# Layer 0's mixer in a two-layer decoder: seven products taken to seven block products each, and decays with a bias per head

## The chip, the cores and the metric

The kernel runs on one core of a Trainium2 chip. The metric is device time in microseconds (us) of one execution, the median of several. The engines are named as in the profile: PE is TensorE's matrix multiplication (PEld its weight loads), DVE is VectorE, ACT is ScalarE, POOL is GpSimd, and SP is SyncE, which here issues DMA transfers only. The engines run side by side, each working through its own instructions in order, and wait for each other through semaphores.

## The reference, cut to what matters

Two layers work on 512 tokens of width 1024. Each is a half-step SwiGLU, a mixer, and another half-step SwiGLU. Layer 0's mixer is the one that the change touches: one input projection `w_in` feeds a Mamba-2 group (z, x, B, C, dt) and an mLSTM group (q, k, v, an output gate and two scalar gates), and one output projection takes both results.

```python
def hybrid_mixer(h, w_in, conv_w, ...):
    z, xbc, dt_raw, qm, km, vm, om, ig, fg = split_cols(h @ w_in, HY_SPLITS)
    xbc = jax.nn.silu(causal_dwconv(xbc, conv_w, conv_b))
    xs, bm, cm = split_cols(xbc, (1024, 256, 256))
    dt = jax.nn.softplus(dt_raw + dt_bias)
    y = ssd_chunked(xs, dt, -jnp.exp(a_log), bm, cm, 128) + xs * d_skip
    y = rms_norm((y * jax.nn.silu(z)) in 2 groups of 512, ssd_norm)
    hm = mlstm_chunked(qm, km, vm, ig + igate_bias, fg + fgate_bias, 128)
    hm = rms_norm(hm per head, mlstm_norm) * jax.nn.sigmoid(om)
    return jnp.concatenate([y, hm], -1) @ w_out

# inside ssd_chunked, per chunk of 128 tokens and per head; acs is the running sum of dt * A
Lm = jnp.exp(jnp.where(mask, acs[t] - acs[s], -inf))     # decay from token s to token t
# inside mlstm_chunked
S = (q . k) * jnp.exp(Dm - m_t);  w_inter = jnp.exp(inter - m_t)
```

z, v and the output gate are 1024 columns wide, q and k 512, x with B and C 1536. Everything is float32.

## The kernel before

**Products in three passes.** A float32 factor is split into a rounded high part and the rest (`split`: ACT copies the high part, DVE subtracts it from the source to get the low part), and a product is three matmuls (`mm3`, lines 274 to 279): high times high, high times low, low times high. `form` (line 257) does this for a block of weights: `raw` (line 250) loads a block of 128 x 1024 floats from SP into one of four buffers, and `form` writes its two parts into one of five buffers (`rings`). All of ACT's copies there stand on line 239 of the profile, all of DVE's subtractions on line 242. In the other stages there is a second way (lines 529 to 531): ACT writes the negated high part, a DMA issued by POOL adds the source to it, and ACT writes the high part; this keeps DVE out of it.

**Block products elsewhere.** The SwiGLU stages form most of their products by Winograd's variant of Strassen's scheme: both factors are cut into two by two blocks, and seven products of blocks (`seven`) take the place of eight, at the price of sums and differences of blocks ahead and behind. A block product here is 256 columns by 256 tokens over 512 rows, in matmuls of 256 columns.

**Layer 0's mixer, `hybrid`.** It has two interleavings (`weave`, which issues steps of a second stream between steps of the first) and is then ordered by the framework's scheduler, which fixes each engine's order when the program is built:

- `gates` (the scalar gates and everything derived from them) beside `conv`: six pairs of column groups of x, B and C. Each group takes 24 matmuls of 512 columns (`gemm_feat`), a multiplication of the result by the row of norms `rrow` on DVE (line 1022), the first step of the convolution on POOL, three more on DVE, and Silu on ACT.
- `ssd`, the Mamba recurrence over four chunks and four quarters of the heads, beside `projections`: q and k by columns (`gemm_feat`, line 973 takes them out of PSUM), then v and the output gate by tokens (`gemm_tok`, four banks of PSUM, ACT takes them out with Sigmoid for the gate). `decays` loads a row of running sums (`rows_from`), subtracts a column of them on DVE (line 1244), masks on POOL (line 1245), takes the exponential on ACT (line 1249), and multiplies by C B^T on DVE (line 1250), one quarter ahead.
- `mlstm` beside `gate`: z by columns (line 1046 multiplies by `rrow`), Silu, the product with the Mamba result, and its norm. `mlstm` forms its weights in the same manner (lines 1322 and 1324 subtract) and multiplies the gate by the result head by head (line 1357) and by its norm (line 1381).

Then `project` multiplies the 16 chunks of both results by `w_out` and starts the following SwiGLU. Every engine has one queue; a weight load waits on SP for its buffer, and a sum waits on POOL for ACT's copy.

Of the kernel before, what the change touches and what calls it, by code (L numbers as in the profile page):

```python
# [16 lines left out]
P = 128  # L17
# [27 lines left out]
NMIX = dict(mix0=10, mix1=15)  # L45
# [168 lines left out]
class Trunk:  # L214
# [21 lines left out]
    def split(self, hi, lo, src, eng="act"):  # L236
        nc = self.nc
        if eng == "act":
            nc.scalar.activation(hi, src, AF.Copy)
        else:  # L240
            nc.vector.tensor_copy(hi, src)
        nc.vector.tensor_tensor(lo, src, hi.bitcast(F32), op=ALU.subtract)
# [14 lines left out]
    def form(self, raw):  # L257
# [5 lines left out]
        if self.stage == "mix1":  # L263
# [7 lines left out]
    def wload(self, src):  # L271

        n = src.shape[0] // P
        for k in range(0, n, 4):
            yield self.form(self.raw(src[k * P : (k + 4) * P].rearrange("(k p) n -> p k n", p=P), 4, 256))
# [163 lines left out]

    def spread(self, cols, n, name):  # L440
# [10 lines left out]
    def rows_from(self, src, name):  # L451

        rows = self.tmp.tile([P, 4, P], F32, name=name, tag="rows", bufs=4)
        self.nc.sync.dma_start(rows, src.rearrange("n p -> (n p)").partition_broadcast(P).rearrange("q (n p) -> q n p", p=P))
        return rows
# [316 lines left out]
    def prep_later(self, which, k, last, squares=True, half=None):  # L772
# [5 lines left out]
        if k == 0 and not half:  # L778
            self.which = which
            self.xgn = [[Lazy(lambda: self.part.tile([P, 4, T], F32R, name="xgn", tag="xg")) for _ in range(2)] for _ in range(2)]  # L780
            squares4 = Lazy(lambda: self.tmp.tile([P, 4, T], F32, name="ssq", tag="ssq", bufs=1))
# [165 lines left out]
    def hybrid(self, nxt):  # L947
# [6 lines left out]
        weave(  # L954
            self.gates(w, ((0, DT0, 16), (16, F0, 4), (20, I0, 4)), g),
            chain(*(self.conv(w, X0, cp, xs, bc) for cp in (4, 5, 0, 1, 2, 3))),
            1.0,
        )

        q, k = self.slot("q"), self.slot("k")  # L960
        v = self.tmp.tile([P, 2, 2, 4, 257], F32, name="v", tag="v", bufs=1)
        v = [v[:, i] for i in range(2)]
        og = []

        def projections():
            for t, c0, sc in ((q, Q0, 128 ** -0.5), (k, K0, 1.0)):
                for cp in range(2):
                    W = self.wload(w[:, c0 + cp * 256 : c0 + cp * 256 + 256])
                    W = list(W)
                    for m in range(2):  # L970
                        ps = self.mmps("pqk")
                        self.gemm_feat(ps, W, m)
                        self.mark = nc.vector.scalar_tensor_tensor(
                            t[:, 2 * cp + m], ps, sc, self.rrow, op0=ALU.mult, op1=ALU.mult
                        )
                        yield
            for t in v:
                with self.tc.issue_after(self.mark.ins):
                    nc.vector.memset(t[:, :, :, 256:257], 1.0)
            for h in (0, 2):  # L980
                yield from self.gemm_tok(w, V0 + h * 256, 512, lambda b, ps, h=h: nc.scalar.activation(
                    v[b // 2][:, b % 2, h : h + 2, 0:256], ps.rearrange("p (h n) -> p h n", h=2), AF.Copy,
                    scale=self.rcol[:, b : b + 1]))
            og.extend(self.slot("og", F32, (2, 4, 256)) for _ in range(2))
            for h in (0, 2):
                yield from self.gemm_tok(w, O0 + h * 256, 512, lambda b, ps, h=h: nc.scalar.activation(
                    og[b // 2][:, b % 2, h : h + 2], ps.rearrange("p (h n) -> p h n", h=2), AF.Sigmoid,
                    scale=self.rcol[:, b : b + 1]))

        weave(self.ssd(xs, bc, g), projections(), 1.35)  # L990

        hid = [None] * 16

        def mlstm():
            yield from self.mlstm(q, k, v, og, g)
            hh, hl = self.feat("hh", KC, F32R), self.feat("hl", KC, F32R)
            for c in range(KC):
                pt = self.aux("pht", (T,))
                for b in range(NB):
                    nc.tensor.transpose(  # L1000
                        pt[:, b * P : (b + 1) * P], og[b // 2][:, b % 2, c // 2, (c % 2) * P : (c % 2 + 1) * P],
                        self.ident,
                    )
                self.split_gain(hh[c], hl[c], pt, self.par[:, 116 + c : 117 + c])
                hid[KC + c] = (hh[c], hl[c])
                if c % 2:
                    yield
# [26 lines left out]
    def gate(self, w, Z0, xs, hid):  # L1034

        nc = self.nc
        for grp in range(2):
            for cp in range(2):
                c0 = Z0 + grp * 512 + cp * 256
                W = list(self.wload(w[:, c0 : c0 + 256]))  # L1040
                for m in range(2):
                    c = 4 * grp + 2 * cp + m
# [851 lines left out]
```

## Time and profile before

| | us |
|---|---|
| median of 3 runs (2020.55 to 2025.87) | 2020.58 |
| the profiled execution | 2019.29 |
| its span in the trace | 2017.6 |
| TensorE busy in the span | 1984.4 |
| VectorE busy | 1581.4 |
| ScalarE busy | 1170.2 |
| GpSimd busy | 270.1 |

Layer 0's mixer lies between about 353 and 762 us of the span. Its last matmul of x, B and C starts at 431.0, that of q and k at 485.3, of v and the gate at 595.3, of z at 664.4, and of the output projection at 756.3. [...] In tables of stretches each engine has its busy time and, in brackets, its number of instructions; PEclk is the clock granted to TensorE as a part of the full one. In tables of groups a row has the line, engine, operation, result and sources, shape and count, then busy time in us and mean ns of one, then the engine's idle time just before them and what ended it.

### The profile page before, as it was taken

To read this page: it belongs to the slowest core of one execution; us is meant where nothing else is said; L and a number is where in the kernel's file an instruction comes from. 1 tells how busy PE (TensorE), PEld (TensorE's weight loads), DVE (VectorE), ACT (ScalarE), POOL (GpSimd) and SP (SyncE) were. 2 spreads that over 40 slices of the span, in tenths; PEclk is the share of its full clock that TensorE was granted. 3 is DMA by queue.
4 is the path that set the end of the run, shared out by engine and by line. 5 is a ranking of instruction groups with operands and counts; after the bars stand their busy time and mean duration, and the time that the engine had idled before them with its cause. 6 is when DMAs were issued, how large, how long until landed. Compare 5 with 4: busy or idle time off the path is not lost.

```text
span 2017.6 us, 34412 instructions
## 1 busy us (share of the span) xinstructions
PE 1984.4 (98%) x13892; PEld 1800.6 (89%) x13892; DVE 1581.4 (78%) x2340; ACT 1170.2 (58%) x1716; POOL 270.1 (13%) x335
## 2 busy tenths in 40 slices
PE   8999999999999999999999999999999999999998
PEld 6999999787788888999998899999965678999998
DVE  6898878886547648988888898978679847988886
ACT  6666657442345434666565575756667644757565
POOL 1000101321101011010002010101215321101010
PEclk9999999999999999999999999999899999999999
DMA  7556566433331232666565356656754202656564
GB/s 210 136 148 167 150 164 148 125 107 115 103 96 63 82 97 63 168 157 162 155 152 149 94 148 167 161 153 160 191 116 105 53 16 69 157 158 165 150 168 115
DMA packets 214439, 265.49 MB, mean 132 GB/s; under 512 B 14140, under 2 KB 187400, under 8 KB 214280
## 3 DMA queue, kind: packets, MB, share of 16 engines
q1 hardware_dynamic: 193632, 190.87, 30.5%
q0 software_dynamic: 20448, 72.36, 19.2%
q8 instruction: 109, 1.79, 0.4%
q14 instruction: 50, 0.41, 0.1%
q10 hardware_dynamic: 200, 0.06, 0.0%
HBM read 188.77 MB, written 2.14 MB: 95 GB/s over the span
## 4 chain that ended last, share of the span: by engine, by line
PE 86%; DVE 5%; DMA 4%; issue 2%; ACT 1%; POOL 1%; SPq 0%; ACTq 0%; POOLq 0%; DVEq 0%
PE pA L281 9%; PE pA L280 9%; PE pA L282 9%; PE pD L280 5%; PE pD L281 5%; PE pD L282 5%; PE pB L280 2%; PE pB L281 2%; PE pB L282 2%; DMA form<-raw 2%; PE po L280 2%; PE po L282 2%; PE po L281 2%; PE ptok L280 2%; PE pu L282 2%
## 5 line engine op out<-in xcount | busy, mean ns | idle before, releaser
L502 DVE TENSOR_TENSOR form<-raw,form 128x1024 fp32r<-128x1024 f32 (+1 forms) x327 | 388.0, 1191 | 113.2 <-ACT form L500 112.3
L500 ACT ACTIVATE form<-raw 128x1024 fp32r<-128x1024 f32 (+1 forms) x327 | 334.6, 1027 | 177.3 <-DVE raw L495 120.6
L280 PE MATMUL pA<-xf,form 128*128 128x256 f32 x1152 | 322.1, 280 | 0.0
L281 PE MATMUL pA<-xf,form 128*128 128x256 f32 x1152 | 321.8, 279 | 0.0
L282 PE MATMUL pA<-xf,form 128*128 128x256 f32 x1152 | 321.4, 279 | 0.0
L495 DVE TENSOR_TENSOR raw<-raw 128x1024 f32<-128x1024 f32 (+2 forms) x241 | 283.6, 1180 | 17.4 <-DMA raw<-in_ffn_w_down 8.6
L530 POOL DMA_DIRECT2D form<-raw x136 | 116.9, 860 | 1202.7 <-ACT form L529 1142.4
L529 ACT ACTIVATE form<-raw 128x1024 fp32r<-128x1024 f32 (+1 forms) x136 | 140.1, 1031 | 140.3 <-PE pD L282 77.4
L280 PEld LDWEIGHTS pA<-xf,form 128*128 128x128 f32 x1152 | 216.4, 188 | 0.2
L282 PEld LDWEIGHTS pA<-xf,form 128*128 128x128 f32 x1152 | 216.1, 188 | 0.0
L281 PEld LDWEIGHTS pA<-xf,form 128*128 128x128 f32 x1152 | 215.8, 187 | 0.2
L281 PE MATMUL pA<-hid,form 128*128 128x256 f32 x704 | 198.6, 282 | 2.8 <-DVE hid L502 2.8
L280 PE MATMUL pA<-hid,form 128*128 128x256 f32 x704 | 198.8, 282 | 0.5 <-ACT hid L500 0.4
L282 PE MATMUL pA<-hid,form 128*128 128x256 f32 x704 | 197.4, 280 | 0.0
L280 PE MATMUL pD<-xf,form 128*128 128x256 f32 x576 | 161.2, 280 | 0.0
L281 PE MATMUL pD<-xf,form 128*128 128x256 f32 x576 | 161.2, 280 | 0.0
L282 PE MATMUL pD<-xf,form 128*128 128x256 f32 x576 | 161.0, 280 | 0.0
L495 DVE TENSOR_TENSOR ft<-ft 128x256 f32<-128x256 f32 (+2 forms) x288 | 146.1, 539 | 4.6 <-ACT ft L748 1.2
L531 ACT ACTIVATE form<-raw 128x1024 fp32r<-128x1024 f32 (+1 forms) x136 | 138.6, 1021 | 0.0
L281 PEld LDWEIGHTS pA<-hid,form 128*128 128x128 f32 x704 | 132.3, 188 | 4.7 <-DVE hid L502 4.6
L280 PEld LDWEIGHTS pA<-hid,form 128*128 128x128 f32 x704 | 132.6, 188 | 1.3 <-ACT hid L500 0.6
L282 PEld LDWEIGHTS pA<-hid,form 128*128 128x128 f32 x704 | 132.3, 188 | 0.0
(447 smaller groups left out, 5191.5 us busy)
## 6 DMA issues: line engine op xcount, KB each, us to landing
form<-raw POOLq DMA_DIRECT2D x120, 512.0 KB, 5.6
raw<-in_ffn_w_gate SPq DMA_DIRECT2D x88, 512.0 KB, 3.8
raw<-in_ffn_w_up SPq DMA_DIRECT2D x88, 512.0 KB, 4.0
raw<-in_ffn_w_down SPq DMA_DIRECT2D x64, 512.0 KB, 4.4
raw<-in_hy_w_in SPq DMA_DIRECT2D x44, 512.0 KB, 3.5
raw<-in_ffn_w_down SPq DMA_DIRECT2D x32, 384.0 KB, 3.4
raw<-in_hy_w_out SPq DMA_DIRECT2D x16, 512.0 KB, 3.3
form<-raw POOLq DMA_DIRECT2D x16, 384.0 KB, 4.2
```

The costliest lines, as they stand in the source:

```text
L280: mm(out, l[0], r[0], start=start, stop=False)
L281: mm(out, l[0], r[1], start=False, stop=False)
L282: mm(out, l[1], r[0], start=False, stop=stop)
L495: (self.p if pool else self.v)(n, lambda: e.tensor_tensor(out(), x(), y(), op=op), reads, writes)
L500: self.s(n, lambda: nc.scalar.activation(hi(), src(), AF.Copy), srck, hik)
L502: n, lambda: nc.vector.tensor_tensor(lo(), src(), hi().bitcast(F32), op=ALU.subtract), srck + hik, lok
L529: self.s(n, lambda: nc.scalar.activation(f()[:, 1], raw, AF.Copy, scale=-1.0), rawk, lok)
L530: self.plan.add("gpsimd", 0.85, lambda: nc.gpsimd.dma_start(f()[:, 1], raw, accum_op=ALU.add), rawk + lok, lok, 5.5)
L531: self.s(n, lambda: nc.scalar.activation(f()[:, 0], raw, AF.Copy), rawk, hik)
```

## The change

Seven of the mixer's products, each 512 columns (or tokens) by 512 tokens (or columns) over 1024 rows, become block products: two for v, one for k, two for z, two for the output gate. The convolution's products and q stay as they were and now come first, together with the gates.

- `xforms_now` makes the seven forms of the activations once: normalized blocks, four sums or differences per quarter, and seven splits, 28 in all, of 256 columns.
- `seven_now` is the new product: four loads, four differences of weight blocks on DVE (line 1100), seven forms. The sixth and seventh form (`f12`, `f21`) are made by ACT, POOL's DMA and ACT. Three pairs of PSUM banks come from two buffers; of the four results, three are a sum of two pairs (ACT keeps one, DVE adds), one is copied by ACT.
- `wload` makes the second half of the weights of the convolution and of q in the same way while `early` is set.
- Since the activations are normalized beforehand, multiplications by `rrow` and `rcol` behind these products go.
- In `decays` and in `mlstm`'s `weights` the subtraction goes, and the exponential of 512 columns becomes four of 128 with a bias (and a scale) per head. `ssd` runs two quarters ahead instead of one.
- The output gate comes last: `mlstm` leaves its unnormalized result in `v` and its norms in `rs`, and `output_gate` multiplies both in one step. z runs beside `mlstm`, and `project` takes z's two halves first.
- Work tiles move into one tile `rooms`; the normalized activations get a place of their own.

```diff
-            self.split(f[:, 0], f[:, 1], raw)           # form: always, in this stage
+        if self.stage == "mix0" and self.summing:
+            nc.scalar.activation(f[:, 1], raw, AF.Copy, scale=-1.0)
+            nc.gpsimd.dma_start(f[:, 1], raw, accum_op=ALU.add)
+            nc.scalar.activation(f[:, 0], raw, AF.Copy)
+        else:
+            self.split(f[:, 0], f[:, 1], raw)
...
-        weave(self.ssd(xs, bc, g), projections(), 1.35)     # q, k, v, output gate
-        weave(mlstm(), self.gate(w, Z0, xs, hid), 0.8)
-        self.project(a["hy_w_out"][0], hid, 1.0, nxt, ((0, 4), (8, 16), (4, 8)), 2)
+        weave(gates, early, 1.0)                            # early: convolution, q
+        weave(early, self.xforms_now(xf), 0.4)
+        weave(self.ssd(xs, bc, g), values(), 1.8)           # v, v, k
+        weave(mlstm, zgate, 1.5)
+        drain(output_gate())
+        self.project(a["hy_w_out"][0], hid, 1.0, nxt, ((0, 4), (4, 8), (8, 16)), 2)
...
+    def xforms_now(self, xf):
+        for q in range(4):
+            for m in range(2):
+                nc.vector.scalar_tensor_tensor(t[:, 2 * m : 2 * m + 2], xT[2 * q + m], gain, row, op0=ALU.mult, op1=ALU.mult)
+            tt(t[:, 4], t[:, 1], t[:, 3], op=ALU.add)
+            tt(t[:, 5], t[:, 4], t[:, 0], op=ALU.subtract)
+            tt(t[:, 6], t[:, 0], t[:, 1], op=ALU.subtract)
+            tt(t[:, 7], t[:, 2], t[:, 5], op=ALU.subtract)
+            for form, i in (...):                           # seven forms
+                self.ready = self.split(tiles[form][:, 0, q], tiles[form][:, 1, q], t[:, i])
...
+    def seven_now(self, w, c0, xf, rows, keep, done):
+        keep(0, mul(A, made(b11), self.A11, True))
+        done(0, 0, mul(B, made(b21), self.A12, True))
+        less(b11, b12, b11)
+        less(b12, b22, b12)
+        f22 = made(b22)
+        less(b22, b22, b11)
+        keep(1, mul(A, made(b22), self.S2, False))
+        less(b21, b21, b22)
+        keep(2, mul(D, made(b11), self.S1, True))
+        f12, f21 = made(b12, True), made(b21, True)
+        done(1, 1, mul(A, f12, self.S3, False))
+        done(0, 1, mul(D, f22, self.S4, False))
+        done(1, 0, mul(A, f21, self.A22, False))
...
-            tt(e, rows, g["acs"][:, c, hs].unsqueeze(2).to_broadcast([P, 4, P]), op=ALU.subtract)
             nc.gpsimd.affine_select(out=e, in_=e, ...)
-            nc.scalar.activation(e, e, AF.Exp)
+            for j in range(4):
+                nc.scalar.activation(e[:, j], rows[:, j], AF.Exp, bias=g["nacs"][:, c, 4 * q + j : 4 * q + j + 1])
...
-                tt(oc[:, h], oc[:, h], pn[:, 0:256], op=ALU.mult)                # mlstm, per head
-            tt(oc, oc, r.unsqueeze(2).to_broadcast([P, 4, 256]), op=ALU.mult)
+                nc.scalar.activation(vc[:, h, 0:256], pn[:, 0:256], AF.Copy)
+            rs.append(r)
```

More of the change, by code (lines that the diff above doesn't have):

```diff
@@ L1290, in ssd, with mlstm @@
         block(0)
[L1291 removed]
+        ahead = [decays(0, 0)]
         for i, (c, q) in enumerate(steps):
[L1293 to L1297 removed]
+            while len(ahead) < 3 and i + len(ahead) < len(steps):
+                c1, q1 = steps[i + len(ahead)]
+                if not q1:
+                    block(c1)
+                ahead.append(decays(c1, q1))
             yield
[L1299 removed]
+            outputs(c, q, *ahead.pop(0))
             if q == 3 and c < NB - 1:
                 st = state(c)
[L1303 removed]
+    def mlstm(self, q, k, v, rs, g):
         nc = self.nc
         tt = nc.vector.tensor_tensor
[L1307 removed]
+        ktok = [self.room("ktok", 4, P) for _ in range(NB - 1)]
         st = None
```

316 lines of the change are left out of this document (181 added, 135 removed).

## The prediction

> **What bounds the kernel now.** The page's first part was read first, then the busy times by stretch, which single out the stage that the change touches.
>
> ```profile
> PE 1984.4 (98%) x13892; PEld 1800.6 (89%) x13892; DVE 1581.4 (78%) x2340; ACT 1170.2 (58%) x1716; POOL 270.1 (13%) x335
> ```
>
> ```profile
> core 0: us, PE busy (x) PEld busy (x) DVE busy (x) ACT busy (x) POOL busy (x), PEclk, DMA share, GB/s
> 379.40:431.00 51.60, 51.60 (x231) 42.13 (x231) 48.00 (x89) 21.86 (x27) 15.59 (x11) 1.00 0.30 93
> 431.00:486.00 55.00, 55.00 (x290) 43.36 (x290) 39.11 (x68) 21.39 (x30) 9.02 (x8) 1.00 0.38 120
> 486.00:596.00 110.00, 110.00 (x595) 85.56 (x590) 56.88 (x87) 44.23 (x60) 11.48 (x12) 1.00 0.34 108
> 596.00:664.00 68.00, 68.00 (x336) 57.46 (x335) 49.94 (x105) 33.03 (x81) 6.72 (x6) 1.00 0.16 55
> 180.00:240.00 60.00, 60.00 (x510) 59.96 (x509) 53.71 (x69) 40.75 (x55) 5.16 (x6) 1.00 0.64 166
> 880.00:960.00 80.00, 80.00 (x681) 80.00 (x681) 66.91 (x81) 52.41 (x69) 7.68 (x9) 1.00 0.67 165
> ```
>
> The first four stretches are layer 0's mixer: convolution, q and k, values and output gate, z with the mLSTM. TensorE is busy without a gap in all of them at a granted clock of 1.00. So the stage lasts as long as its matmuls, and what VectorE (DVE) and ScalarE (ACT) do there is free as long as they keep up. The last two rows are SwiGLU stretches that already run block products: TensorE without a gap beside a VectorE at 90% (53.71 of 60) and 84%.
>
> **TensorE's saving.** Start to start, 512 columns against 256:
>
> ```profile
> 598.66 0.39 PE L282 MATMUL pz<-xgn,form 128*128 128x512 f32 x1
> 601.40 0.39 PE L282 MATMUL pz<-xgn,form 128*128 128x512 f32 x1
> 104.33 0.28 PE L280 MATMUL pA<-xf,form 128*128 128x256 f32 x1
> 106.34 0.28 PE L282 MATMUL pA<-hid,form 128*128 128x256 f32 x1
> ```
>
> There are 12 steps between the first two rows, 0.2283 us each, and 17 between the others, 0.1182 us each. A 512x512x1024 product is 96 matmuls of 512 columns now (21.92 us) and 168 of 256 after (7 block products x 2 x 4 x 3; 19.86 us). Seven products change (k, two of v, two of z, two of the gate): 7 x 2.06 = 14.4 us less. The small matmuls of the recurrences keep their count, but for two transposes. [...]
>
> **What VectorE takes on.** Rows of the work that goes:
>
> ```profile
> L242 DVE TENSOR_TENSOR form<-raw,form 128x1024 fp32r<-128x1024 f32 x60 | 74.3, 1240 | 48.5 <-ACT form L239 46.6 <-PE pxd L1225 1.5
> L1244 DVE TENSOR_TENSOR arow<-arow,raw 128x512 f32<-128x512 f32 x16 | 12.2, 765 | 3.4 <-DMA arow<-arows 2.5 <-ACT ce L1242 0.9
> L1324 DVE TENSOR_TENSOR mrow<-raw,mrow 128x512 f32<-128x512 f32 x4 | 3.2, 796 | 0.0
> L1322 DVE TENSOR_TENSOR qs<-raw,mrow 128x512 f32<-128x512 f32 x3 | 2.1, 684 | 0.0
> L1357 DVE TENSOR_TENSOR og<-og,pn 128x256 f32<-128x256 f32 x16 | 6.4, 416 | 4.8 <-ACT hsq L1356 4.8
> L1381 DVE TENSOR_TENSOR og<-og,gev 128x1024 f32<-128x1024 f32 x4 | 4.9, 1220 | 0.0
> L1046 DVE TENSOR_TENSOR t<-pz,raw 128x512 f32<-128x512 f32 x8 | 5.5, 686 | 3.9 <-PE pz L282 3.9
> L1048 DVE TENSOR_TENSOR xs<-xs,t 128x512 f32<-128x512 f32 x8 | 5.5, 689 | 2.9 <-ACT t L1047 2.9
> L1055 DVE TENSOR_TENSOR ssq<-ssq,sq 128x512 f32<-128x512 f32 x6 | 4.4, 736 | 1.4 <-ACT sq L1054 1.4
> L973 DVE SCALAR_TENSOR_TENSOR k<-pqk,raw 128x512 f32<-128x512 f32 x4 | 2.8, 688 | 3.9 <-PE pqk L282 3.9
> ```
>
> and of the same kinds of work elsewhere that comes:
>
> ```profile
> L495 DVE TENSOR_TENSOR raw<-raw 128x1024 f32<-128x1024 f32 x208 | 253.2, 1220 | 16.4 <-DMA raw<-in_ffn_w_down 7.7 <-DMA raw<-in_ffn_w_up 6.7
> L495 DVE TENSOR_TENSOR ft<-pA,ft 128x512 f32<-128x512 f32 x60 | 41.4, 691 | 35.9 <-PE pA L282 35.3
> L495 DVE TENSOR_TENSOR ft<-ft 128x256 f32<-128x256 f32 x176 | 67.8, 421 | 2.5
> L582 DVE SCALAR_TENSOR_TENSOR ft<-raw 128x512 f32<-128x512 f32 x32 | 22.2, 747 | 18.2 <-ACT raw L768 18.2
> L502 DVE TENSOR_TENSOR hid<-ft,hid 128x256 fp32r<-128x256 f32 x44 | 18.4, 418 | 0.0
> ```
>
> Gone: all of the rows from L1244 on (47.0), and one of 44 splits of weights (1.2; the 16 of convolution and q halve to 8 because their second halves go to DMA sums, the products need 35 instead of 28). Added: 28 block differences (34.2), 21 sums out of PSUM (14.5), for z eight products of 512 and twelve sums of 256 (10.6), for the gate sixteen scalings of 256 (6.7), and the seven forms of the activations, 8 x 0.747 + 16 x 0.421 + 28 x 0.418 = 24.4. That is +90.4 - 48.2 = 42.2 us. The four mixer rows sum to 193.9 us in 284.6; with eight splits of the mixers' results that now fall ahead of the output projection (6.0, row below) it becomes 242 in 284.6 - 14.4 = 270.2: 90%, what the SwiGLU rows show as bearable on average. The question is where it bunches.
>
> ```profile
> L386 DVE SCALAR_TENSOR_TENSOR yl<-xs,raw,yh 128x512 fp32r<-128x512 f32 x8 | 5.6, 745 | 0.0
> ```
>
> *Before the first block product.* VectorE's queue opens when the row of norms is there:
>
> ```profile
> 378.22 1.23 DVE L242 TENSOR_TENSOR form<-raw,form 128x1024 fp32r<-128x1024 f32 x1 [5.85 <-ACT form L239]
> 379.36 0.68 DVE L1022 TENSOR_TENSOR u<-pxbc,raw 128x512 f32<-128x512 f32 x1
> 379.96 0.67 DVE L1115 TENSOR_TENSOR gt<-pgate,raw 24x512 f32<-24x512 f32 x1
> ```
>
> Back to back a 1024-wide pass takes 1.14 us, a 512-wide one 0.60, some 0.08 less than their durations. By the compiled order the fourth q must leave PSUM before the second pair of the first product can start, at about 453.6 on TensorE's own pace: 74.2 us after 379.4. Until then VectorE has the 48.0 us of the first row, the forms (24.4 - 52 x 0.08 = 20.3), four differences and three splits of v (8.0), q's four (2.4), the convolution's rest (some 5: one gain, six steps), less five splits (5.7): 78.0; instruction by instruction in that order I get 73.1. At the 93% that the first row reached (48.00 of 51.60) that is 78.6 to 83.9, 4.4 to 9.7 us late; without idle time, nothing. TensorE has nothing else queued in between, so the lateness is paid. I take 4.4.
>
> *The gate's two products.* They run with no recurrence beside them: 39.7 us of TensorE. VectorE needs 2 x (9 x 1.14 + 3 x 0.61 + 8 x 0.34) = 29.6 plus some 10 of z's last gains and splits: 39.6, at 93% 42.6, so 2.9 late (bounds 0 and 7). Values, k and z have 27 to 32 us of VectorE beside 30 to 35 of TensorE; counted the same way; taken at nothing, for the recurrence's matmuls fill what is late (bounds 0 and 5 in all).
>
> **Transfers and queues.**
>
> ```profile
> form<-raw POOLq DMA_DIRECT2D x120, 512.0 KB, 5.6
> raw<-in_hy_w_in SPq DMA_DIRECT2D x44, 512.0 KB, 3.5
> L530 POOL DMA_DIRECT2D form<-raw x136 | 116.9, 860 | 1202.7 <-ACT form L529 1142.4
> ```
>
> SP's weight loads keep number and size. POOL gets 22 more sums of 0.86 us (8 among the convolution's steps, 14 in the products): each waits on POOL for ACT's negated copy, and the convolution's next step or the next masking waits behind it; POOL is busy 15.6 of 51.6 us there, 22.5 with eight more. A raw buffer is free again after load 3.5, split 2.3, difference 1.2, copy 1.1, issue 0.9, landing 5.6: 14.6 us against 19.9 per product, so 5 us of queueing stay hidden. Cost nothing, bound 5 us for each gate product.
>
> **Sum.** -14.4 + 4.4 + 2.9 = -7.1. The profiled execution took 2019.29 us (span 2017.6 and 1.7 around it) and would take 2012.2; the median, 2020.58, lies 1.29 above it: 2013.5.
>
> **Rivals.** *All hidden:* VectorE leaves no gaps where it is late, as it fills up when work is there: 2020.58 - 14.4 = 2006.2. For it, the first row's 93% includes waits that new work can fill.
>
> *ACT becomes the bound beside z:*
>
> ```profile
> L239 ACT ACTIVATE form<-raw 128x1024 fp32r<-128x1024 f32 x60 | 63.2, 1057 | 114.0 <-PE ptok L282 34.3 <-PE po L281 29.7 <-PE pxbc L281 15.4
> L1249 ACT ACTIVATE arow<-arow 128x512 f32<-128x512 f32 x16 | 10.0, 628 | 22.6 <-POOL arow L1245 22.6
> L1356 ACT ACTIVATE hsq<-pn 128x256 f32<-128x256 f32 x16 | 6.0, 377 | 0.0
> L1472 ACT ACTIVATE keys<-pq 128x128 f32<-128x128 f32 x4 | 1.1, 274 | 0.6 <-PE pq L1466 0.6
> L1731 ACT ACTIVATE pn<-pn,raw,keep 128x128 f32<-128x128 f32 x16 | 7.7, 482 | 0.0
> ```
>
> Its 33.0 us grow by ten copies of weights (10.6), six evacuations (3.8), sixteen copies of 256 (6.0), and seven exponentials of 512 that become 28 of 128, at 274 ns (no bias) to 482 (bias, scale and accumulator): 3.3 to 9.1. So 56.7 to 62.5 beside 68 - 4.1 = 63.9; if it too leaves 7% of its time idle, the upper end takes 67.2, and 3.3 us come on top of the forecast: 2016.8. [...]
>
> *VectorE's waits, the slower side:*
>
> ```profile
> L1268 DVE SCALAR_TENSOR_TENSOR xs<-xs,raw,py 128x128 f32<-128x128 f32 x32 | 9.5, 343 | 22.4 <-PE py L1265 22.4
> ```
>
> It works in order. L242's row shows 48.5 us idle ahead of 60 splits, 0.81 each; 43 splits at that make 35, and this row has 22 more for the recurrence, 57 together. In 270.2 us with 242 of work 28 fit; past 28 each is paid, past 42 the change loses. At 57 it is 29 - 14.4 = +14.6: 2035. Against it: with work queued, 379.4 to 431 left 3.6 us idle.
>
> That the products are not blocked or not summed by DMA the compiled order excludes.
>
> **Chances and range.** Forecast 0.32, all hidden 0.18, ACT 0.24, VectorE's waits 0.26. The first two are faster by over 0.3% (6.1 us, about what a measurement of this kernel can tell), ACT is no change, the last slower. The range goes from 2005.5, all hidden, to 2028, two thirds of the way from the forecast to the last rival, which leaves about 0.13 above it.
>
> **What would show it.** Right: stretches of pw matmuls at 0.118 us per step; VectorE over 90% busy from 380 to 450; TensorE's gaps of 3 to 10 us ended by q's evacuation or a form ahead of the first product, and some in the gate's. All hidden: no gaps. ACT: gaps beside z ended by ACT. Waits: gaps all over the stage, ended by a VectorE that itself waited for ACT. Wrong altogether: gaps for DMA sums, or a change outside the mixer.

## The result, and the profile after

The changed kernel takes 2047.43 us (median of 4 runs, 2045.30 to 2050.36) beside 2020.57 for the kernel before (4 runs, 2018.37 to 2025.87). The ratio is 1.013, with a 95% interval of 1.0106 to 1.0154: slower, and outside the predicted range of 2005.5 to 2028. The profiled execution took 2048.88 us, 2047.1 of it in the span.

The changed kernel's page, first part, and then the busy times by stretch: convolution, q with the activations' forms, the two products of v, k, z's two, the gate's two, output projection. The columns are those of the prediction's first table: the stretch and its length, busy time and number of instructions of PE, PEld, DVE, ACT and POOL, the granted clock, the DMA engines' busy share and GB/s.

```profile
PE 1980.5 (97%) x14394; PEld 1824.7 (89%) x14394; DVE 1617.9 (79%) x2409; ACT 1243.1 (61%) x1888; POOL 298.3 (15%) x357
```

```profile
380.00:432.50 52.50, 52.50 (x229) 42.06 (x228) 50.77 (x106) 30.82 (x51) 18.32 (x14) 1.00 0.49 131
432.50:455.00 22.50, 22.50 (x98) 18.15 (x97) 21.90 (x37) 6.83 (x10) 8.67 (x4) 1.00 0.19 47
455.00:521.40 66.40, 58.31 (x487) 53.77 (x486) 44.38 (x86) 40.05 (x82) 11.26 (x14) 0.97 0.52 136
521.40:560.00 38.60, 33.01 (x263) 30.12 (x264) 28.31 (x40) 19.32 (x37) 10.93 (x7) 0.91 0.43 116
560.00:642.20 82.20, 72.36 (x530) 66.52 (x529) 57.10 (x102) 63.75 (x148) 13.65 (x12) 0.96 0.36 93
642.20:706.00 63.80, 56.34 (x401) 53.80 (x400) 41.26 (x68) 34.23 (x49) 6.74 (x7) 0.92 0.52 133
706.00:788.00 82.00, 82.00 (x370) 68.06 (x369) 36.79 (x44) 28.31 (x36) 7.58 (x6) 1.00 0.33 104
```

TensorE is without a gap up to the first block products and again in the output projection. Between them, in four stretches that last 251 us, it is idle for 8.1 + 5.6 + 9.8 + 7.5 = 31.0 us, and it runs at a granted clock of 0.91 to 0.97 where it had 1.00 before. VectorE, which I had expected to be the tight engine, is busy 65 to 73% there, ScalarE 50 to 78%. No engine is full; they wait for each other.

The loss adds up, with the forecast saving taken as given. The saving of 14.4 us alone would have given 2006.2, so 41.3 us were lost. TensorE's busy time would have been 1984.4 - 14.4 = 1970.0; it is 1980.5, so 10.5 us are put down to matmuls at a lower clock. With the 31.0 us of idle time that makes 41.5.

The waits in 455 to 706 (engine and line, what it waited for: us in total, times, longest), TensorE's first, then ACT's, then those of SyncE's queue:

```profile
PE pw L281 <- ACT form L239: 8.2, 5, 4.5
PE pw L281 <- ACT rooms L1031: 7.8, 4, 4.2
PE py L1367 <- DVE rooms L1354: 6.4, 1, 6.4
PE pw L281 <- ACT rooms L1002: 3.1, 1, 3.1
```

```profile
ACT rooms L1346 <- DMA rooms<-arows: 24.8, 8, 7.8
ACT rooms L1353 <- POOL rooms L1348: 11.9, 6, 4.4
```

```profile
SPq L254 <- DVE raw L1100: 58.5, 5, 24.2
SPq L254 <- DMA form<-raw: 56.1, 14, 8.2
SPq L254 <- DVE form L242: 32.0, 4, 18.0
```

TensorE waits for ACT: for a form (L239), or for the copy that takes a block product out of PSUM (L1031, L1002). ACT in turn waits in its own order for other things: for the recurrences' rows, and for the masks on POOL that follow them. Before the change ACT's longest total wait in this place was for TensorE (34.3 us in 12 waits). SyncE's weight loads waited 56.1 us, in 14 waits, for a DMA sum to land, and 90.5 us for VectorE's differences and splits. A load that waits is not yet a loss: what counts is whether its block is there when its turn comes. The transfers had become slower too (from issue to landing, in us, in 455 to 700, where before it was 3.5 for weights and 3.9 for either kind of rows):

```profile
raw<-in_hy_w_in SPq DMA_DIRECT2D x24, 512.0 KB, 5.0
form<-raw POOLq DMA_DIRECT2D x14, 512.0 KB, 5.7
rooms<-arows SPq DMA_DIRECT2D x16, 256.0 KB, 7.2
rooms<-mrows SPq DMA_DIRECT2D x4, 256.0 KB, 7.4
```

How a gap comes about is seen in the longest one, by the timelines of SyncE's queue, ACT, DVE and PE (start, length, what ended the idle time before it in brackets):

```profile
568.01 0.32 SPq L471 DMA_DIRECT2D rooms<-arows  x1
```

```profile
570.05 0.58 ACT L1031 ACTIVATE rooms<-pw 128x512 f32<-128x512 f32 x1
575.80 0.63 ACT L1346 ACTIVATE rooms<-rooms 128x512 f32<-128x512 f32 x1 [5.17 <-DMA rooms<-arows]
576.45 1.28 ACT L1040 ACT_TABLE_LOAD   x1
...
578.39 1.28 ACT L1431 ACT_TABLE_LOAD   x1
...
580.87 1.26 ACT L1353 ACTIVATE rooms<-rooms,raw 128x128 f32<-128x128 f32 x4
```

```profile
582.24 0.69 DVE L1354 TENSOR_TENSOR rooms<-rooms 128x512 f32<-128x512 f32 x1 [0.55 <-POOL rooms L1433]
```

```profile
583.07 0.70 PE L1367 MATMUL py<-rooms 128*64 128x128 f32 x4 [6.37 <-DVE rooms L1354]
```

A rows load issued at 568.0 lands 7.8 us later, and the mLSTM's rows, issued at 568.9, after 9.5. ACT stands at the first for 5.17 us with everything behind it; then come z's Silu and the mLSTM's exponentials with a table load of 1.28 us each, and only then the decay (L1353) that DVE and TensorE need. TensorE's row names DVE, which had done nothing wrong. The rows load did not stand behind a sum: the weight load ahead of it in SyncE's queue had waited 10.9 us for a split on VectorE. With the late landing goes that everything came at once: from 569 to 576 the DMA engines were full (a share of 0.99 to 1.12 in each microsecond), with weights, rows and two sums that took 8.1 and 8.6 us to land.

The next three gaps of TensorE do not all begin so. The one of 4.5 us up to 534.3 begins at a mask on GpSimd that took 4.75 us, with ACT standing at it; behind it come ACT's exponentials and a sum's two copies (1.9 us) before the form that TensorE needs:

```profile
525.32 4.75 POOL L1348 TENSOR_SCALAR_AFFINE_SELECT rooms<-rooms 128x512 f32<-128x512 f32 x1 [5.96 <-ACT rooms L1346]
530.11 1.27 ACT L1353 ACTIVATE rooms<-rooms,raw 128x128 f32<-128x128 f32 x4 [4.37 <-POOL rooms L1348]
```

In the one of 4.2 us up to 663.2, between the gate's two products, ACT stands 7.8 us at a weight load, and between 640 and 664 SyncE's loads wait 12.6 us for the two sums: here a load did stand behind a sum. In the one of 3.1 us up to 506.8, ACT stands 4.6 us at rows that land in 5.1 us, with the DMA engines at a share of 0.97 from 500 to 505. These four make 18.2 of the 31.0 us.

### The profile page after: what moved, and what is told of

Its sections match the earlier page's. It is cut to its first block, busy times and chain, and to the rows that moved or that the text cites. A ratio compares the mean times of both kernels' runs of the same rounds, so it can differ in the third digit from the quotient of the medians.

```text
span 2047.1 us, 35746 instructions
## 1 busy us (share of the span) xinstructions
PE 1980.5 (97%) x14394; PEld 1824.7 (89%) x14394; DVE 1617.9 (79%) x2409; ACT 1243.1 (61%) x1888; POOL 298.3 (15%) x357
## 4 chain that ended last, share of the span: by engine, by line
PE 77%; DMA 9%; DVE 6%; issue 3%; ACT 3%; POOL 1%; SPq 0%; ACTq 0%; POOLq 0%; DVEq 0%
PE pA L282 9%; PE pA L281 9%; PE pA L283 9%; PE pD L281 4%; PE pD L283 4%; PE pD L282 4%; DMA form<-raw 3%; PE pB L281 2%; PE pB L283 2%; PE pB L282 2%; DMA raw<-in_ffn_w_down 2%; PE po L281 2%; PE po L283 2%; PE po L282 2%; PE pu L281 1%
## 5 line engine op out<-in xcount | busy, mean ns | idle before, releaser
L281 PEld LDWEIGHTS pA<-xf,form 128*128 128x128 f32 x1152 | 218.9, 190 | 0.4 <-DVE ft L512 0.3
L282 PEld LDWEIGHTS pA<-xf,form 128*128 128x128 f32 x1152 | 218.9, 190 | 0.2
L283 PEld LDWEIGHTS pA<-xf,form 128*128 128x128 f32 x1152 | 218.8, 190 | 0.0
L282 PEld LDWEIGHTS pA<-hid,form 128*128 128x128 f32 x704 | 132.9, 189 | 5.8 <-DVE hid L519 5.8
L281 PEld LDWEIGHTS pA<-hid,form 128*128 128x128 f32 x704 | 133.0, 189 | 2.3 <-ACT hid L517 1.3
L663 ACT ACTIVATE ft<-pA 128x512 f32<-128x512 f32 x120 | 71.5, 596 | 102.9 <-PE pA L283 91.6
```

The lines of the kernel that those rows point to most:

```text
L281: mm(out, l[0], r[0], start=start, stop=False)
L282: mm(out, l[0], r[1], start=False, stop=False)
L283: mm(out, l[1], r[0], start=False, stop=stop)
L663: self.s(T, lambda: nc.scalar.activation(to(), ps()[:, :, 0:H], AF.Copy), [(*psk, 0), (*psk, 1)], tok)
```

## The experiments

Theory 1: a product's four raw buffers are held until its sums have landed, and the next weights come late. Rivals: VectorE's waits in order (2), ACT's work (3), the rows on SyncE's queue (4), and later form buffers (5), PSUM's accumulators (6), a chain over SyncE's queue (7), and the two parts of a sum (8, 9). Ratios are to the kernel before on the same chip, with 95% intervals; the changed kernel has 1.0130. Differences in us are between medians; the groups of runs were on different chips, where the kernel before had medians of 2018.5 to 2020.6, so that by the ratios a difference can come out one to three us otherwise.

### First four: one suspect each

**a_nosum**: `f12, f21 = made(b12), made(b21)` instead of `made(b12, True), made(b21, True)`.

> The two low parts of each block product that a DMA sum makes (b12, b21) are made on VectorE like the other five; nothing else differs from the changed kernel (2047.4 us; its mixer lost about 31 us of TensorE's time in gaps and 12 in lower granted clock behind them). Theory 1 (a block product's raw buffers are held until the sums have landed, and the next product's weights are loaded only then): a raw buffer is free some 6 us earlier (0.9 issue and 5.6 landing against a 1.2 us pass), at the six boundaries between products 20 to 40 us: 2008 to 2027. Theory 2 (VectorE's waits in order): 14 passes of 1.14 more on VectorE, 16 us: 2050 to 2063. Theory 3 (ACT is late): 14 copies of 1.05 less on ACT: 2033 to 2047. Theory 4 (the recurrences' rows, loaded on the same SyncE queue, hold back the weights and stop POOL and ACT): within 6 us of 2047.

Measured: 2026.82 us, 1.0036 (1.0019 to 1.0052). The 14 sums of the products cost 20.6 us (19 by the ratios), half of what was lost. Against theory 2, 16 us more on VectorE did no harm on balance. The rows' landing and ACT's waits for rows and masks without sums:

```profile
rooms<-arows SPq DMA_DIRECT2D x16, 256.0 KB, 3.9
```

```profile
ACT rooms L1353 <- POOL rooms L1348: 15.2, 12, 3.4
ACT rooms L1346 <- DMA rooms<-arows: 7.2, 5, 2.4
```

The rows land in 3.9 us instead of 7.2, and ACT waits 7.2 us for them instead of 24.8. SyncE's weight loads, though, wait as long as before, 139.7 us at splits and differences where it was 146.6 with the sums:

```profile
SPq L254 <- DVE form L242: 75.4, 19, 17.9
SPq L254 <- DVE raw L1100: 64.3, 5, 30.1
```

So the 56.1 us that loads stood at sums are no measure of what the sums cost.

**a_early**: the sums asked for earlier.

```diff
         less(b12, b22, b12)
+        f12 = made(b12, True)
         f22 = made(b22)
...
         less(b21, b21, b22)
+        f21 = made(b21, True)
         keep(2, mul(D, made(b11), self.S1, True))
-        f12, f21 = made(b12, True), made(b21, True)
```

> The same instructions as in the changed kernel, but each DMA sum is asked for as soon as its difference is made, before the second and third block products instead of behind them. Theory 1: the sums land two block products (5.7 us) earlier, and the next product's loads start earlier by as much at six boundaries: 2013 to 2030. Theories 2, 3 and 4: same instructions, so within 6 us of 2047.

Measured: 2038.98 us, 1.0097 (1.0074 to 1.0120): 8.5 us less by the medians, some third of what theory 1 asked for and more than its rivals allow; the interval just meets that of the changed kernel. ACT waits 9.9 us for rows here (455 to 690; 7.2 without sums, 24.8 in the changed kernel), yet the kernel stays 12 us behind a_nosum.

**a_norows**: `rows` is a view of other numbers in SBUF, and the 20 loads of L471 go, so that this kernel computes other decays.

> Leaves out the 20 loads of the recurrences' rows of decays (the decays are computed from other numbers in SBUF, with another bias), everything else as in the changed kernel. Theory 4: SyncE's queue has only weights, POOL's masks and ACT's exponentials wait for no landing (24.8 us of ACT's waits were for rows): 2015 to 2030. Theory 1: the buffers are still held by the sums: 2038 to 2047. Theories 2 and 3: within 6 us of 2047.

Measured: 2040.44 us, 1.0097 (1.0072 to 1.0122): 7.0 us less, and here too the interval just meets that of the changed kernel. The rows are at most one of the places where TensorE is made to wait: without any of them most of the loss is still there.

**a_exp1**: in `decays`, one addition on VectorE and one exponential of 512.

```diff
-            for j in range(4):
-                nc.scalar.activation(e[:, j], rows[:, j], AF.Exp, bias=g["nacs"][:, c, 4 * q + j : 4 * q + j + 1])
+            tt(e, e, g["nacs"][:, c, hs].unsqueeze(2).to_broadcast([P, 4, P]), op=ALU.add)
+            nc.scalar.activation(e, e, AF.Exp)
```

> The Mamba decays by one exponential of 512 columns behind an addition on VectorE, as in the kernel before, everything else as in the changed kernel: ACT has 16 x (1.25 - 0.63) = 10 us less to do, VectorE 16 x 0.77 = 12 us more. Theory 3 (ACT is late): 2035 to 2042. Theory 2 (VectorE): 2050 to 2060. Theories 1 and 4: within 6 us of 2047.

Measured: 2045.28 us, 1.0127 (1.0103 to 1.0151). The Mamba exponentials with a bias per head cost nothing that could be measured against the form before; theory 3 is out as far as this work goes.

### Second four: the buffers

**b_rot**: the raw buffers are dealt out in another turn.

```diff
-        b11, b21, b12, b22 = (self.raw(...) ...)     # always buffers 0, 1, 2, 3 in turn
+        o = self.count.get("slots") or [(turn + i) % 4 for i in range(4)]
+        self.count["slots"] = [o[3], o[0], o[2], o[1]]
+        b11, b21, b12, b22 = (block(i) for i in range(4))    # loads into slots[o[i]]
```

> The same instructions as in the changed kernel (2047.4 us), DMA sums included; only the raw buffers are dealt out in another turn: a product's first and second weight block go into the buffers of the last product's b22 and b11, which no sum reads, its third and fourth into those of b12 and b21, which the sums read. Theory 1 (weights wait for buffers that sums hold): the first two blocks of each product no longer wait for a landing; most of the 20 us that the sums cost (2026.8 without them) comes back: 2024 to 2034. If instead the sums' own lateness stops TensorE and ACT (low parts that land too late for their block): within 6 us of 2047.

Measured: 2051.50 us, 1.0151 (1.0121 to 1.0180). No gain. The trace showed why it was not yet a verdict: SyncE's weight loads still waited 62.6 us for sums in 14 waits from 455 to 700, and a gap of 6.58 us stood in the gate's products.

**b_rot_nosum**: the edits of b_rot and a_nosum together.

> The other turn of the raw buffers and no DMA sums in the products. If the buffers' hold is the rest of the loss as well (in the kernel without sums SyncE's weight loads still waited 64 us for differences and 61 us for splits): 2008 to 2018. If that kernel's rest comes from VectorE (18 us of waits at its evacuations and differences) or from the rows: 2022 to 2030.

Measured: 2030.43 us, 1.0048 (1.0030 to 1.0067), as without the turn. Dealing the raw buffers out otherwise brings nothing once the sums are gone.

**b_rot_swap_nosum**: besides, `done(0, 1, mul(D, f22, self.S4, False))` stands ahead of `done(1, 1, mul(A, f12, self.S3, False))`.

> As the one before, and the fifth and sixth block product change places (f22 with S4 ahead of f12 with S3), so that the form buffer that the next product's first block takes over is read one block product (2.8 us) earlier. Theory 5 (the five form buffers: the first form of a product can begin only in the last block product of the one before, 2.3 us of ACT and VectorE in 2.8): 6 to 12 us below the run before. Otherwise equal to it within 4 us.

Measured: 2031.86 us, 1.0050 (1.0029 to 1.0071). The form buffers of theory 5 are not it: 6 to 12 us less were expected, none came.

**b_rsn_pool**: besides, `nc.gpsimd.dma_start` for the rows instead of `nc.sync.dma_start`.

> As the one before, and the recurrences' rows are loaded from GpSimd's queue instead of SyncE's, so that no weight load stands behind a rows load that waits for a room. Theory 4: 4 to 10 us below the run before. If rows are only a second waiter: within 4 us, or above it since POOL's masks then stand behind the loads.

Measured: 2030.00 us, 1.0060 (1.0040 to 1.0081): no gain.

### Third four: accumulators, VectorE, the queue of the rows

**c_p4**: from a_nosum, four accumulators of one PSUM bank instead of two of two banks.

```diff
-        pair = lambda: self.ps_two.tile([P, 2, T], F32, name="pw", tag="pA")
+        pair = lambda: self.ps_two.tile([P, 2, H], F32, name="pw", tag="pW", bufs=4)
```

> From the kernel without DMA sums in the products (2026.8 us): the block products' partial results lie in four PSUM tiles of one bank instead of two tiles of two banks, so that a product's third accumulator does not wait for VectorE's first sum and the next product's first not for the last evacuation. Theory 6 (two accumulators): some 8 of the 18 us of TensorE's gaps there were ended by these evacuations, with the lower clock behind them 8 to 14 us: 2013 to 2019. If VectorE and ACT are late anyway, the next wait behind it takes over: within 4 us of 2026.8.

Measured: 2020.41 us, 1.0002 (0.9987 to 1.0017): 6.4 us below a_nosum, with intervals that do not meet. In this kernel and in c_p4_poold each half of a bank has a start mark of its own, and both compute other results than the kernel before; all instructions are there, and d_ns_p4_rs, with one mark per bank (and with the turn and the exchange, which had brought nothing alone), takes the same time. Theory 6 holds for the kernel without sums.

**c_poold**: from a_nosum, two of four differences as `nc.gpsimd.tensor_tensor(..., op=ALU.subtract)`.

> From the kernel without DMA sums in the products (2026.8 us): two of each product's four block differences run on GpSimd instead of VectorE (14 passes of 1.2 us less there, 17 us of the 188 that it works in the 232 us from the first block product to the output projection). Theory 2 (VectorE in order is the rest of the loss): 2014 to 2022. If GpSimd's pass of 1024 is as slow as its sums of 512 elsewhere (1.58 us each), a difference takes about 3 us and its low part waits for it: 2027 to 2037.

Measured: 2037.14 us, 1.0094 (1.0075 to 1.0113), 10.3 us more. By line and form, GpSimd's differences (count, busy us, mean ns):

```profile
L1135 POOL TENSOR_TENSOR raw<-raw 128x1024 f32<-128x1024 f32 x7 | 20.4, 2918 | 18.5 <-DVE raw L1100 9.4 <-issue 6.2 <-ACT form L239 2.9
L1129 POOL TENSOR_TENSOR raw<-raw 128x1024 f32<-128x1024 f32 x6 | 18.6, 3101 | 36.2 <-DVE raw L1100 32.0 <-DVE gev L1485 4.2
```

At 2.9 to 3.1 us in the mean for 1.2 on VectorE, with a form waiting for each, this says nothing for or against VectorE as the rest of the loss.

**c_p4_poold**: the edits of c_p4 and c_poold together.

> Both of the edits before. If theories 2 and 6 both hold: 2006 to 2016, below the kernel before. If only one does: that one's time.

Measured: 2032.29 us, 1.0059 (1.0041 to 1.0076): c_p4 with GpSimd's cost on top.

**c_rows_pool**: the changed kernel with the rows on GpSimd's queue.

> From the changed kernel (2047.4 us), sums kept: the recurrences' rows are loaded from GpSimd's queue instead of SyncE's. Theory 7 (a chain: a sum that lands late holds a weight load, SyncE's queue holds the rows behind it, these hold POOL's mask, ACT's exponentials and with them ACT's copies for the block products): the chain is cut at its second link: 2030 to 2041, as without the rows (2040.4). If the sums act otherwise: within 6 us of 2047, or above it since sums then stand behind rows that wait for a room.

Measured: 2054.78 us, 1.0176 (1.0159 to 1.0193), 7.4 us more: POOL's queue now has rows that wait for a room, with sums and masks behind them, and ACT waits 14.1 us for masks in 10 waits from 455 to 690 (11.9 in 6 in the changed kernel). It doesn't cut the chain of theory 7, it moves it to another queue; the theory is neither shown nor refuted by it.

### Fourth four: buffers and accumulators together

**d_rot_early**: b_rot's turn and a_early's order.

> The changed kernel's instructions with both of the edits that alone gave 8 us or nothing: raw buffers dealt out so that a product's first two blocks go where no sum reads, and each sum asked for as soon as its difference is made, so that the buffers of the third and fourth block are free before the product ends. Theory 1 (the hold of raw buffers, by whichever block waits for it): as without sums, 2024 to 2032. If the sums cost by their copies on ACT or by traffic: like the early sums alone, 2036 to 2044.

Measured: 2040.97 us, 1.0110 (1.0094 to 1.0127), as a_early alone. But the hold was still there (SyncE's queue, from 455 to 706):

```profile
SPq L1108 <- DMA form<-raw: 77.6, 10, 24.9
SPq L254 <- DMA form<-raw: 24.8, 2, 21.9
```

The weight loads stood 102 us behind landing sums, in 12 waits. The edit freed the first two blocks and not the queue: each later load waits for a sum in its order, and what follows waits behind it. So it is no clean test of theory 1.

**d_p4_sums**: c_p4's edit in the changed kernel, and `start and q == 0 and s == 0`, one start mark per bank.

> From the changed kernel, sums kept: four PSUM accumulators of one bank each, and one start mark for a bank (the first half's; the second half's first matmul goes without). If the accumulators are a cause of their own: 6 us less, 2038 to 2044. If they matter only once the sums are gone: within 4 us of 2047.

Measured: 2042.32 us, 1.0114 (1.0096 to 1.0133). 5.1 us less by the medians, but the interval overlaps that of the changed kernel by more than those of a_early and a_norows: inconclusive.

**d_ns_p4_rs**: a_nosum, four accumulators with one mark, b_rot's turn, the exchange.

> No sums in the products, four accumulators with the single start mark, raw buffers dealt out anew and the fifth and sixth block product exchanged. Without the last two edits 2020.4, where 5.6 of 10 us of gaps lay at the gate's second product, whose weights came late. If buffers are that rest: 2008 to 2016, below the kernel before. If VectorE is (it has 188 us of work in 219): within 4 us of 2020.

Measured: 2019.59 us, 1.0003 (0.9986 to 1.0019), equal to c_p4 and to the kernel before. The page's first part, and the stretch of the gate's two products:

```profile
PE 1972.0 (98%) x14394; PEld 1819.4 (90%) x14394; DVE 1634.5 (81%) x2423; ACT 1228.8 (61%) x1872; POOL 285.7 (14%) x343
```

```profile
630.00:668.00 38.00, 34.42 (x272) 33.03 (x271) 35.61 (x61) 26.05 (x45) 3.90 (x3) 1.00 0.29 84
```

The same 14,394 matmuls take 1972.0 us instead of 1980.5, as the clock stays up (0.99 from 455 to 700). TensorE's saving against 1984.4 is there, 12.4 us; idle time takes nearly all of it. In the gate's products VectorE is now busy 35.61 of 38 us, as full as the prediction had feared. It is not shown to be the bound there: TensorE's named waits in this stretch are 3.2 us at ACT and 0.4 at VectorE.

**d_all_sums**: with sums, the turn, the early order and four accumulators.

> The changed kernel with its sums, raw buffers dealt out anew, early sums and four accumulators. If theories 1 and 6 hold, VectorE has 17 us less to do than without sums and nothing waits: 2006 to 2018. If the sums cost otherwise: 2030 to 2040.

Measured: 2035.51 us, 1.0080 (1.0063 to 1.0097). Every arrangement tried leaves the sums 10 us or more behind the nearest kernel without them (10.5 for d_rot_early against b_rot_nosum, 15.9 here against d_ns_p4_rs). In both of these the rows land in a median of 3.4 us, so what remains of the sums' cost is not the rows' landing.

### Last two: the parts of a sum

**e_copies**: from a_nosum, ACT's negated copy ahead of each of the 14 splits, without the transfer.

```diff
+            if summed:
+                nc.scalar.activation(f1, block, AF.Copy, scale=-1.0)     # f1: the low part's place
             return self.form(block)
```

> From the kernel without sums in the products (2026.8 us): ahead of each of the 14 splits that a sum did before, ACT writes one more negated copy of the block (14 x 1.05 = 15 us of ACT, as with the sums), which VectorE's pass then overwrites; no transfer. Theory 8 (the sums cost by ACT's work in order): 2038 to 2047. If ACT has room: within 4 us of 2026.8.

Measured: 2032.35 us, 1.0075 (1.0042 to 1.0108): 5.5 us more by the medians, 8 by the ratios, a quarter to two fifths of the sums' cost; the interval still touches that of a_nosum.

**e_moves**: from a_nosum, a transfer of the same size on GpSimd's queue behind each split, with no product waiting for it.

```diff
+            if summed:
+                nc.gpsimd.dma_start(aside, f[0])      # aside: in DRAM
```

> From the kernel without sums in the products (2026.8 us): behind each of the same 14 splits, GpSimd's queue issues a transfer of 512 KB (the high part, out to memory, which nobody reads), so POOL has the 14 issues and the DMA queues the traffic, and no product waits for it but by the form buffer it reads. Theory 9 (the sums cost by POOL's issues ahead of the masks and by traffic that delays the rows' landing, 7.2 us with sums and 3.9 without): 2036 to 2047. If neither: within 4 us of 2026.8; then, if the copies cost nothing either, it is the length of the sum's own chain, 8 us instead of 2.3.

Measured: 2027.32 us, 1.0045 (1.0026 to 1.0064): 0.5 us more by the medians, 2 by the ratios. Issues and copies out to memory cost next to nothing here. But these transfers are lighter than sums: from 455 to 700 the DMA engines' share is 0.41, beside 0.33 in a_nosum and 0.45 in the changed kernel, where the sums took 16.9% of their time, and ACT waits 12.8 us for rows, not 24.8. So theory 9 is out for POOL's issues, and stays open for the traffic of the sums themselves; theory 8 holds for a part at most.

## Why the prediction was wrong

**TensorE's saving: there, and 2 us smaller than forecast.** 14.4 us were forecast; with the clock kept up, 12.4 show in busy time. The step from the start of a matmul of 256 columns to that of the next (the rows, 0.28 us long, overlap) was taken from a SwiGLU stage, 0.1182 us. In these products it is 0.1197, by 35 steps of d_ns_p4_rs:

```profile
643.40 0.28 PE L281 MATMUL pw<-form,xf 128*128 128x256 f32 x1
647.59 0.28 PE L283 MATMUL pw<-form,xf 128*128 128x256 f32 x1
```

At that, 168 of them take 20.1 us, a product saves 1.8, and seven save 12.7.

**VectorE's work: right in amount.** Forecast 242 us from the convolution to the gate; the six stretches above sum to 50.77 + 21.90 + 44.38 + 28.31 + 57.10 + 41.26 = 243.7. *Before the first block product* nothing was late, though VectorE is busy 97% from 380 to 455: TensorE has no gap there, so the 4.4 us were not paid, and the range's end of zero held. *The gate's products* lost 7.5 us of idle time, but beside a VectorE at 65%, so the 2.9 us forecast for a VectorE that is late are not what was lost there; without sums and with four accumulators VectorE is 94% busy there, and TensorE's waits still name ACT.

**"Transfers and queues ... Cost nothing, bound 5 us for each gate product": the step that failed.** It added up one buffer's cycle, 14.6 us against 19.9 us of TensorE, and called the rest slack. That sum held the durations of a chain in which nobody waits, and each landing as long as before. Taking the sums out of the seven products gave back 20.6 us, shown by a_nosum: a term put at nothing, with 10 us as its bound for the two gate products, cost about 20. How it costs that is argued only. In the run the links of the cycle belong to queues that work in order: a negated copy stands in ACT's queue behind what waits for rows, the sum in POOL's waits for the copy, a load in SyncE's for the sum, the rows behind the load. And transfers that came together landed late: 5.0 us instead of 3.5 for weights, 7.2 instead of 3.9 for rows. Of the four longest gaps, one begins at a load behind a sum, two at rows that landed late beside full DMA engines, and one at a slow mask on GpSimd, as a_nosum has them too (up to 3.73 us). Of the 20 us the copies on ACT bring some 5.5 to 8, and issues and lighter transfers 0.5 to 2. The other 9 to 15 are left for the sum's own landing and traffic, by elimination: no run removed the wait and kept the sums, and none kept their traffic without the wait. Which link is the dearest stays open. The direct test of theory 1, more raw buffers, was not tried.

**Not in the sum at all: two accumulators.** The prediction never asked who waits for a block product's evacuation from PSUM, though three of them share two places. Worth 6.4 us without the sums (c_p4 against a_nosum); with the sums it is not shown (d_p4_sums).

**Not in the sum either: the clock.** Each idle microsecond was counted once; 8.5 us came on top (1980.5 against the 1972.0 of d_ns_p4_rs, 10.5 if the whole forecast saving is taken as a base), put down to matmuls at a granted clock of 0.50 behind the gaps of 4.2, 4.5 and 6.4 us. Behind that of 4.5, rows of small matmuls (L1367, L1369) start 0.43 us apart (536.3 to 537.6); at 1.00 they start 0.22 apart (509.5 to 510.1).

**What is still lost without sums and with four accumulators**, some 14 us against 2006.2, is idle time of 10.7 us in 455 to 700 in d_ns_p4_rs, spread over gaps of 0.4 to 3 us that end at ACT or DVE, some 2 us of saving that the longer step took, and a little clock. It was not taken apart further, and no version tried beats the kernel before.

**The rivals.** *All hidden* (2006.2) was right ahead of the first block product, where no gap came, and nowhere else. *ACT becomes the bound beside z*: its work grew about as priced (63.75 us against 56.7 to 62.5, the exponential with a bias 389 ns by its row below), but in 82.2 us, 78% of them; undoing the Mamba exponentials brought nothing. The rival's sign, gaps beside z that end at ACT, showed in 2.1 us only; the gap of 6.4 us there ends at a VectorE that waited for ACT, which had itself stood at rows.

```profile
L1353 ACT ACTIVATE rooms<-rooms,raw 128x128 f32<-128x128 f32 x64 | 20.1, 389 | 11.9 <-POOL rooms L1348 11.9
L242 DVE TENSOR_TENSOR form<-raw,form 128x1024 fp32r<-128x1024 f32 x44 | 53.8, 1224 | 24.1 <-ACT form L239 18.0 <-PE prow L438 5.9
L1100 DVE TENSOR_TENSOR raw<-raw 128x1024 f32<-128x1024 f32 x28 | 34.0, 1214 | 0.0
```

*VectorE's waits* (2035) came nearest in time and had the right idea, waits in an in-order queue, on the wrong engine: L242 waits 24.1 us ahead of 44 splits, 0.55 each where the rival took 0.81, and L1100 never. Going over to VectorE for the low parts made the kernel faster, not slower. The line "wrong altogether: gaps for DMA sums" named what a_nosum then found, but not as it can be seen: no row of TensorE's waits in this stage names a DMA, as the engine that it stood at had itself waited for something else.

## What to carry to other kernels

Before a transfer that replaces work on an engine is put at nothing, list who is queued behind each instruction that waits for it, and what else the DMA engines carry at that time, not only the cycle of the buffer. VectorE, which the sums were to spare, had room for the 14 splits here. Where TensorE's gaps end at an engine that is two thirds busy, look at what that engine itself stood at, and then take the suspected source out whole; shifting its buffers or its order showed little here. Count accumulators and their evacuations like any other buffer, and price a long gap (here those of 4.2, 4.5 and 6.4 us) with the slow matmuls behind it. A long wait in a queue of loads proves nothing by itself: take its source out and see whether the time moves.

## What the runs showed of the hardware

**The longest gaps were paid again in clock.** Stretches around two gaps of the changed kernel, the mean granted clock after POOL's column, first a gap of 4.5 us, then one of 3.1:

```profile
529.70:534.20 4.50, 0.04 (x1) 0.00 (x0) 2.71 (x5) 4.09 (x7) 1.24 (x2) 0.82 0.41 121
534.20:536.00 1.80, 1.72 (x12) 1.50 (x14) 1.80 (x2) 0.82 (x2) 0.00 (x0) 0.50 1.06 207
536.00:538.00 2.00, 2.00 (x20) 2.00 (x17) 0.85 (x3) 1.21 (x2) 0.85 (x1) 0.50 0.34 66
538.00:540.00 2.00, 2.00 (x13) 1.67 (x12) 0.94 (x3) 0.00 (x0) 0.00 (x0) 0.65 1.02 193
```

```profile
503.60:506.80 3.20, 0.06 (x2) 0.04 (x1) 0.55 (x1) 1.21 (x3) 0.51 (x1) 1.00 0.29 57
506.80:508.80 2.00, 2.00 (x17) 1.87 (x18) 1.86 (x3) 2.00 (x3) 0.64 (x1) 1.00 0.00 0
```

After the gap of 4.5 us the clock was 0.50 for over 4 us; after that of 3.1 us it stayed at 1.00. It was 0.50 too from 583.0 to 587.0, behind the gap of 6.4 us, and from 663.2 to 669.0, behind that of 4.2. These rows fix no limit: d_ns_p4_rs has a mean clock of 0.95 from 560 to 630, with gaps of 3.10 and 1.63 us as its longest there.

**A mask on GpSimd took 4.76 us instead of 0.63 beside a VectorE at work.** In b_rot, two masks of the same size on POOL, VectorE's passes during the second, and who waited for it:

```profile
500.03 0.63 POOL L1355 TENSOR_SCALAR_AFFINE_SELECT rooms<-rooms 128x512 f32<-128x512 f32 x1 [1.97 <-ACT rooms L1353]
533.78 4.76 POOL L1355 TENSOR_SCALAR_AFFINE_SELECT rooms<-rooms 128x512 f32<-128x512 f32 x1 [5.78 <-ACT rooms L1353]
```

```profile
533.96 1.22 DVE L1100 TENSOR_TENSOR raw<-raw 128x1024 f32<-128x1024 f32 x1
535.09 1.22 DVE L242 TENSOR_TENSOR form<-raw,form 128x1024 fp32r<-128x1024 f32 x1
536.23 0.69 DVE L1364 TENSOR_TENSOR rooms<-rooms,bc 128x512 f32<-128x512 f32 x1
536.83 1.22 DVE L1100 TENSOR_TENSOR raw<-raw 128x1024 f32<-128x1024 f32 x1
```

```profile
538.58 1.28 ACT L1360 ACTIVATE rooms<-rooms,raw 128x128 f32<-128x128 f32 x4 [4.37 <-POOL rooms L1355]
```

VectorE runs passes with two inputs from SBUF back to back until 538.0; the mask ends at 538.5, and ACT had stood at it for 4.37 us. What held the mask up no run shows, and not every mask beside such passes took that long: the one at 491.57 took 0.70 us beside L1361 and L1364 of VectorE (491.08 to 492.81). The mask of 4.75 us in the changed kernel stood beside five such passes from 524.4 to 529.6. In the kernel before no mask from 430 to 706 took more than 2.11 us.

**Two start marks in one PSUM bank gave other results.** With two halves of one bank, each started by itself (c_p4, c_p4_poold), the kernel computed other results; with one mark for the bank (d_p4_sums, d_ns_p4_rs, d_all_sums) it computed those of the kernel before. What the second mark does inside the bank is not shown.
